# A decoder layer's expert retrieval: a shorter routing spread over the first expert half, and the first four queries computed with tokens on partitions

## Chip, cores and metric

One core of a Trainium2 chip runs the whole layer. The metric is the device time of one execution in microseconds (us); the median of three runs is given, and one more execution was profiled. The core's engines run side by side, each through its own queue in order: PE (matrix products and transposes), DVE (VectorE), ACT (ScalarE), POOL (GpSimd) and SP, which issues the transfers. PE's clock has two levels, 1.2 and 2.4 GHz; the profile gives the granted clock of a stretch as a share of the upper one.

## The reference

256 tokens of 1024 numbers go through a mixer (a state-space part and attention, one output projection), a layer norm, and a PEER sublayer, then a second norm. The change lies in the first norm and in PEER:

```python
h = _layernorm(DN_ALPHA * h + mix, ln1_g, ln1_b)
# PEER, per chunk of 128 tokens (8 heads, two key halves of 128 keys, top 16)
q = (xc @ w_q).reshape(TOKEN_CHUNK, 8, 2, 128)
s = jnp.einsum('thcd,hcnd->thcn', q, sub_keys)
s1, i1 = lax.top_k(s[:, :, 0], 16)
s2, i2 = lax.top_k(s[:, :, 1], 16)
cand = (s1[..., :, None] + s2[..., None, :]).reshape(TOKEN_CHUNK, 8, 256)
cidx = (i1[..., :, None] * 128 + i2[..., None, :]).reshape(TOKEN_CHUNK, 8, 256)
top, pos = lax.top_k(cand, 16)
eidx = jnp.take_along_axis(cidx, pos, axis=-1)
g = jax.nn.softmax(top, axis=-1)
act = jax.nn.gelu(jnp.einsum('td,thkd->thk', xc, expert_u[eidx]))
out = jnp.einsum('thk,thkd->td', g * act, expert_v[eidx])
```

There are 16384 experts, 16 heads-times-halves (called `hc`), all in float32.

## The kernel before

PEER is computed densely: all 16384 experts' products with all 256 tokens are formed, 128 experts at a time (128 `u` tiles, later 128 `v` tiles), and weighted by gates that are zero for experts not chosen. A float32 product is made of three float32r products. Each weight tile of 128 x 1024 is loaded by SP into one of four `raw` buffers; ScalarE rounds it to `hi` (L71, three buffers), and DVE or GpSimd forms the rest, `lo = raw - hi` (L72, three buffers). The normed tokens `xh`, `xl` are split in the same way, with features on partitions. `dense` (L995) then does 24 matmuls of 256 columns: 8 of (hi, xh), 8 of (hi, xl), 8 of (lo, xh).

The stages, in order:
- The norm runs over two blocks of 128 tokens. Block 0: ScalarE centres (L680), GpSimd scales (L681), DVE finishes `h1b` (L684), PE transposes it (L689), ScalarE writes `xh` (L690) and DVE `xl` (L698). Block 1 is the same, with DVE at L677 in place of ScalarE and GpSimd.
- The w_q loop over 16 `hc`: load, split (`lo` on GpSimd for every fourth, on DVE otherwise), `dense`, a copy `qT` by ScalarE (L756), two score matmuls against `keys` (L744), their copies `sco` (L745), and two `top16` on DVE. A `top16` is five operations on 128 values: MAX8, FIND_INDEX8, MATCH_REPLACE8, MAX8, FIND_INDEX8.
- The first half of `u`: 32 calls of `u_pair`, each two tiles and one Gelu of 128 x 512 by ScalarE (L769). The second tile's `lo` is GpSimd's. Between them `route(b)` forms, for each block, the 16 x 16 sums `cand` (L784), eight `top16` on 256 values, and turns the positions into the two key indices by comparisons with a ramp (`eq`, L799 to L804), then the softmax (L808 to L814). It is written one step after each pair, but a scheduler orders each engine's queue by when inputs are ready, and put nearly all of it ahead.
- The second half of `u` with the gates beside it, then the `v` tiles (L925), then the last norm.

Of the kernel before, what the change touches and what calls it, by code (L numbers as in the profile page):

```python
# [20 lines left out]
T = 256  # L21
# [32 lines left out]
def layer(ctx, tc, I, out, tap=None, upto=None):  # L54
# [19 lines left out]

    ident = const.tile([128, 128], F32, name="ident")
# [26 lines left out]

    with ExitStack() as px:
# [6 lines left out]
        with ExitStack() as mx:  # L110
            sb = mx.enter_context(tc.tile_pool(name="sb", bufs=1))
            def eng(g, i):
                return P if CFG[g][i] == "P" else V

            prm = sb.tile([128, 1088], F32, name="prm")
# [25 lines left out]
            U = sb.tile([128, NPAIR, 2, 32], F32, name="U")  # L141
# [142 lines left out]
            big = [sb.tile([128, 1024], F32, name=f"big{n}") for n in range(4)]  # L284
# [60 lines left out]
            def s5_c():  # L345
                tmp = [sb.tile([128, 1024], F32, tag=t, name="cp") for t in ("yT", "dU")]
                powers(Lam, 4, cre, cim, Cbd, 1, -1.0, (eng("cp", 0), eng("cp", 1)), tmp)
# [99 lines left out]
            def glu(yT):  # L447
                yv = yT.rearrange("p k b j c -> p k (b j c)")
                yh = sb.tile([128, 4, T], F32R, tag="big2", name="yh")
                yl = sb.tile([128, 4, T], F32R, tag="big3", name="yl")  # L450
# [97 lines left out]
            def do(w):  # L548
# [63 lines left out]
            if tap:  # L612
# [5 lines left out]
                   allow_small_or_imprecise_dtypes=True)  # L618

# [51 lines left out]
            def ln_apply(b):  # L671
                mean, nstd = st[b]
                z, h1 = gz[:, 2 + b], h1b[:, b]
                for c in range(2):
# [5 lines left out]
                    S.activation(h1[:, cs], z[:, cs], AF.Identity, bias=mean, scale=-1.0)  # L680
                    P.tensor_tensor(h1[:, cs], h1[:, cs], g1[:, 0, cs], op=OP.mult)  # L681
                for c in range(2):
                    cs = slice(512 * c, 512 * c + 512)
                    V.scalar_tensor_tensor(h1[:, cs], h1[:, cs], nstd, g1[:, 1, cs], op0=OP.mult,  # L684
                                           op1=OP.add)
# [4 lines left out]
                    S.copy(xh[:, 4 * c:4 * c + 4, 128 * b:128 * b + 128], pt)  # L690
# [15 lines left out]
            ln_apply(0)  # L706
            ln_stats(1)
# [3 lines left out]
            normed = st["low"]  # L711

# [9 lines left out]
    with ExitStack() as rx:  # L722
# [14 lines left out]
        PACE = lambda i: 1  # L737
        keys = sb.tile([128, 16, NK], F32, name="keys")
        nc.sync.dma_start(keys, I["keys"])
# [9 lines left out]
        late = None  # L749
        for hc in range(16):  # L750
            with tc.issue_after(normed.ins) if hc == 2 else ExitStack():
                hi, lo = split(load(I["w_q"][hc]), P if hc % 4 == 3 else V)
            pt = abank([128, 2, T])[:, 0]
            dense(PE, pt, hi, lo, xh, xl, xl if hc == 0 else lo)
            qT = sb.tile([128, T], F32, tag="qT", bufs=2, name="qT")
            S.copy(qT, pt)  # L756
            if late:
                scores(*late)
            late = hc, qT
        scores(*late)  # L760
# [3 lines left out]
        def u_pair(i):  # L764
            pt = sbank([128, 2, T])
            for r in range(2):
                hi, lo = split(load(I["u"][i + r]), P if r else V)
                dense(PE, pt[:, r], hi, lo, xh, xl)
            S.activation(act[0][:, i:i + 2], pt, AF.Gelu_apprx_tanh)  # L769
# [3 lines left out]
        i2n = sb.tile([128, 2, 128], F32, name="i2n")  # L773

        def route(b):
            for hc in range(EARLY, 16):
                yield top16(tops[b][:, hc], topi[b][:, hc], sco[:, b, hc], NK, "t1")
            topf = sb.tile([128, 16, TOPK], BF, tag="topf", bufs=1, name="topf")
            V.tensor_copy(topf, topi[b])
            cand = sb.tile([128, 8, 16, 16], F32, tag="c0", bufs=1, name="cand")  # L780
            tv = tops[b].rearrange("p (h c) k -> p h c k", c=2)
            fv = topf.rearrange("p (h c) k -> p h c k", c=2)
            sh = [128, 8, 16, 16]
            yield V.tensor_tensor(cand, tv[:, :, 0, :, None].to_broadcast(sh),  # L784
                                  tv[:, :, 1, None, :].to_broadcast(sh), op=OP.add)
            best = sb.tile([128, 8, 16], F32, tag="best", bufs=1, name="best")
# [7 lines left out]
            V.tensor_scalar(ab[:, 0], pos, 4, None, op0=OP.logical_shift_right)  # L794
            V.tensor_scalar(ab[:, 1], pos, 15, None, op0=OP.bitwise_and)
            yield V.tensor_copy(abf, ab)
# [10 lines left out]
            df = sb.tile([128, 8, 16], F32, tag="df", bufs=1, name="df")  # L807
            V.tensor_tensor(df, best, best[:, :, 0:1].to_broadcast([128, 8, 16]), op=OP.subtract)  # L808
            S.activation(df, df, AF.Exp)
            yield  # L810
            sm = sb.tile([128, 8], F32, tag="sm", bufs=1, name="sm")
            V.tensor_reduce(sm, df, axis=AX.X, op=OP.add)
            V.reciprocal(sm, sm)
            yield V.tensor_tensor(gn[:, b].rearrange("p (h k) -> p h k", k=16), df,  # L814
                                  sm[:, :, None].to_broadcast([128, 8, 16]), op=OP.mult)
            pt = sbank([128, 3, 128])
            for i, s in enumerate((i1n, i2n, gn)):
                PE.transpose(pt[:, i], s[:, b], ident)
            sl = slice(128 * b, 128 * b + 128)
            V.tensor_copy(i1T[:, sl], pt[:, 0])  # L820
            V.tensor_copy(i2T[:, sl], pt[:, 1])

            gr = sb.tile([128, 128], F32, tag="gr", bufs=1, name="gr")
            V.tensor_scalar(gr, pt[:, 2], GSC, None, op0=OP.mult)
            V.tensor_copy(gT[:, 0, sl], gr)
            yield V.tensor_sub(gT[:, 1, sl], gr, gT[:, 0, sl])
            if tap:
                tap(f"i1n{b}", i1n[:, b]); tap(f"gn{b}", gn[:, b])
# [6 lines left out]
        for _ in routing:  # L835
# [239 lines left out]
```

## Time and profile before

| what | us |
|---|---|
| runs: median (lowest to highest of 3) | 1005.85 (1005.19 to 1007.71) |
| profiled execution, its own time | 1009.14 |
| its span in the trace | 1007.4 |
| busy: PE, DVE, ACT, POOL | 965.5, 708.8, 453.4, 246.9 |

The span runs from the first to the last instruction that the profiler saw; the execution's own time has about 2 us around it. Busy times of engines overlap, and PE's is not time at its peak.

### The profile page before, as it was taken

Reading aid. Unit: us, or ns where it says so; the run is one execution under the profiler, and the core shown is the slowest. Engines: PE = TensorE matmul, PEld = TensorE weight load, DVE = VectorE, ACT = ScalarE, POOL = GpSimd, SP = SyncE. Lnnn points to the kernel's source line nnn. Section 1 sums busy time; section 2 is a strip of 40 time slices with the busy share of each in tenths; the row PEclk is TensorE's granted clock in tenths of the full one; section 3 lists DMA queues with packets and bytes.
Section 4 is the critical chain, followed back from the end, with each engine's and each line's share of the span. In section 5 each row is a group of like instructions: output and inputs, shape, how many; then the busy total and the mean of one; then the engine's idle time right before and its main releaser. Section 6 shows DMA issues by size and latency. Waiting matters only on the chain.

```text
span 1007.4 us, 16390 instructions
## 1 busy us (share of the span) xinstructions
PE 965.5 (96%) x6326; PEld 857.0 (85%) x6326; DVE 708.8 (70%) x1348; ACT 453.4 (45%) x736; POOL 246.9 (25%) x123
## 2 busy tenths in 40 slices
PE   7899997999889999999999999999999999999996
PEld 3776887999889999999999998978888888888884
DVE  8965577999993612597879999755555555555556
ACT  3214543545344444454444343554554455544552
POOL 2000010144543444345464564600000000000002
PEclk9999998999999999999999999999999999999998
DMA  8312354544446565544444443656666676666661
GB/s 334 105 43 63 95 178 168 162 151 149 149 145 198 167 199 173 165 147 147 147 147 122 133 145 126 209 176 199 190 190 196 196 262 202 190 199 193 191 194 55
DMA packets 46142, 166.24 MB, mean 165 GB/s; under 512 B 5232, under 2 KB 5232, under 8 KB 45936
## 3 DMA queue, kind: packets, MB, share of 16 engines
q1 hardware_dynamic: 46064, 165.20, 51.7%
q8 instruction: 49, 0.80, 0.3%
q14 instruction: 29, 0.24, 0.1%
HBM read 163.09 MB, written 2.10 MB: 164 GB/s over the span
## 4 chain that ended last, share of the span: by engine, by line
PE 71%; DVE 23%; DMA 2%; issue 1%; ACT 1%; SPq 0%; POOL 0%; DVEq 0%; ACTq 0%; POOLq 0%
PE pw L925 34%; PE psb L995 25%; DVE lo L72 5%; PE pw L162 2%; PE pw L873 2%; DVE o L868 2%; DVE act L880 2%; PE psb L151 2%; DVE tmp L732 1%; PE pw L630 1%; DVE o L865 1%; DVE topi L734 1%; DVE eq L801 1%; DMA w<-in_w_in 1%; DVE topi L731 1%
## 5 line engine op out<-in xcount | busy, mean ns | idle before, releaser
L71 ACT CAST hi<-raw 128x1024 fp32r<-128x1024 f32 x275 | 289.6, 1054 | 320.7 <-PE pw L925 164.5
L72 DVE TENSOR_TENSOR lo<-raw,hi 128x1024 fp32r<-128x1024 f32 x207 | 269.2, 1300 | 230.3 <-ACT hi L71 226.8
L72 POOL TENSOR_TENSOR lo<-raw,hi 128x1024 fp32r<-128x1024 f32 x68 | 179.6, 2643 | 184.1 <-ACT hi L71 119.0
L995 PE MATMUL psb<-xh,lo 128*128 128x256 f32 x1024 | 153.0, 289 | 9.9 <-DVE lo L72 9.5
L995 PE MATMUL psb<-xh,hi 128*128 128x256 f32 x1024 | 157.8, 290 | 2.5 <-ACT act L769 2.4
L995 PE MATMUL psb<-xl,hi 128*128 128x256 f32 x1024 | 154.3, 290 | 0.0
L925 PE MATMUL pw<-hi,wh 128*128 128x512 f32 x492 | 151.8, 389 | 1.0 <-ACT wh L845 1.0
L925 PE MATMUL pw<-hi,wl 128*128 128x512 f32 x492 | 152.1, 390 | 0.2
L925 PE MATMUL pw<-lo,wh 128*128 128x512 f32 x492 | 151.7, 389 | 0.0
L995 PEld LDWEIGHTS psb<-xh,lo 128*128 128x128 f32 x1024 | 133.5, 192 | 12.3 <-DVE lo L72 11.9
L995 PEld LDWEIGHTS psb<-xh,hi 128*128 128x128 f32 x1024 | 135.0, 191 | 4.0 <-ACT act L769 3.1
L995 PEld LDWEIGHTS psb<-xl,hi 128*128 128x128 f32 x1024 | 133.5, 192 | 0.0
L925 PEld LDWEIGHTS pw<-hi,wh 128*128 128x128 f32 x492 | 92.3, 188 | 20.5 <-ACT wh L845 1.4
L925 PEld LDWEIGHTS pw<-hi,wl 128*128 128x128 f32 x492 | 92.2, 188 | 20.3 <-DVE wl L846 1.1
L925 PEld LDWEIGHTS pw<-lo,wh 128*128 128x128 f32 x492 | 92.4, 188 | 19.1
L968 POOL TENSOR_TENSOR tail<-tail 128x512 f32<-128x512 f32 x2 | 2.5, 1294 | 345.7 <-ACT tail L967 345.7
L880 DVE SCALAR_TENSOR_TENSOR act<-pw,act 128x256 f32<-128x256 f32 x124 | 65.9, 588 | 20.3 <-PE pw L873 20.3
L883 ACT ACTIVATE act<-pw 128x256 f32<-128x256 f32 (+29 forms) x64 | 27.8, 434 | 102.3 <-DVE act L880 84.5
L873 PE MATMUL pw<-o,o 128*128 128x128 f16 x512 | 72.8, 225 | 0.7 <-DVE o L868 0.7
L909 POOL TENSOR_TENSOR act<-act,ga 128x512 f32<-128x512 f32 (+29 forms) x32 | 51.2, 1600 | 85.5 <-ACT ga L908 64.2
L868 DVE TENSOR_TENSOR o<-eq,gT 128x1024 f16<-128x1024 f16 x64 | 52.4, 855 | 0.1
L846 DVE TENSOR_TENSOR wl<-act,wh 128x256 fp32r<-128x256 f32 x123 | 51.3, 417 | 0.0
(274 smaller groups left out, 992.7 us busy)
## 6 DMA issues: line engine op xcount, KB each, us to landing
raw<-in_u SPq DMA_DIRECT2D x128, 512.0 KB, 3.6
raw<-in_v SPq DMA_DIRECT2D x128, 512.0 KB, 4.1
raw<-in_w_q SPq DMA_DIRECT2D x16, 512.0 KB, 4.1
w<-in_w_in SPq DMA_DIRECT2D x15, 512.0 KB, 8.6
raw<-in_w_out SPq DMA_DIRECT2D x8, 512.0 KB, 4.0
xT<-in_xT SPq DMA_DIRECT2D x4, 256.0 KB, 5.2
raw<-in_w_glu SPq DMA_DIRECT2D x2, 512.0 KB, 3.7
xn<-in_xn SPq DMA_DIRECT2D x2, 512.0 KB, 3.6
```

The source lines that it names most:

```text
L71: S.copy(hi, raw)
L72: eng.tensor_tensor(lo, raw, f32(hi), op=OP.subtract)
L151: PE.matmul(pt[b], xT[:, d, 128 * b:128 * b + 128], w[:, 512 * k:512 * k + 512], start=d == 0, stop=d == 7)
L162: PE.matmul(pt[m], w[:, c], xT[:, d], start=d == 0, stop=d == 7)
L846: V.tensor_sub(wl, act[half][:, i], f32(wh))
L868: V.tensor_tensor(o2[:, k], eq, over(gT[:, k, t]), op=OP.mult)
L873: PE.matmul(pt[:, i], o1[:, (q + i) // 2, :, i % 2], o2[:, k, (q + i) // 2, :, i % 2], start=k == 0, stop=k == 1)
L880: V.scalar_tensor_tensor(a, pt[:, :, HALF * h:HALF * h + n], 1.0 / GSC, a, op0=OP.mult, op1=OP.mult)
L883: S.activation(act[1][:, done:, tq].rearrange("p i t -> p t i"), pt[:, :, HALF + done:], AF.Copy, scale=1.0 / GSC)
L909: P.tensor_tensor(a[:, :, :m1], a[:, :, :m1], raw[:, :, :m1], op=OP.mult)
L925: PE.matmul(acc[b][c], x[:, tk], w[:, 512 * c:512 * c + 512], start=first and j == 0, stop=last and j == 2)
L995: PE.matmul(pt, w[:, 128 * d:128 * d + 128], x[:, d], start=n == 0 and d == 0, stop=n == 2 and d == ND - 1)
```

## The change

It does four things. The weights of the first four queries are loaded as W4 (four pieces of two input slices each, rows of 512 bytes), and `query4(b)` computes these queries for one block with tokens on partitions and the weights moving: 24 matmuls of 512 columns, a copy, four transposes back, a copy. The split of W4's last two pieces is put inside the norm: `hi` on ScalarE behind the centring, `lo` on GpSimd behind block 0's `h1b`. The routing works on 64 candidate pairs in place of 256, finds row and column by short operations, has ScalarE copy the indices out to full size (`fv`), and does one softmax for both blocks. Its 36 steps are tied to the first 26 pairs, each behind the pair's second `lo`; and all `lo` of the first `u` half are DVE's. `keys` is loaded earlier, and some buffers change places.

```diff
+    def split3(raw):
+        hi, lo = (stream.tile([128, 1024], F32R, tag=t, bufs=n, name=t)
+                  for t, n in (("hi", HIB), ("lo", LOB)))
+        S.copy(hi, raw)
+        return hi, lo, V.tensor_tensor(lo, raw, f32(hi), op=OP.subtract)
...
+            W4 = []
+            for q in range(4):
+                raw = stream.tile([128, 1024], F32, tag="raw", bufs=RAWB, name="raw")
+                for k in range(2):
+                    c = 256 * q + 128 * k
+                    st["dma"] = nc.sync.dma_start(
+                        raw[:, 512 * k:512 * k + 512].rearrange("p (h c) -> p h c", h=4),
+                        I["w_q"][0:4, :, c:c + 128].rearrange("h p c -> p h c"))
...
+            def query4(b):
+                tk = slice(128 * b, 128 * b + 128)
+                pt = abank([128, 512])
+                for j, (x, y) in enumerate(((xh, 0), (xh, 1), (xl, 0))):
+                    for d in range(8):
+                        PE.matmul(pt, x[:, d, tk], W4[d // 2][y][:, 512 * (d % 2):512 * (d % 2) + 512],
+                                  start=j == 0 and d == 0, stop=j == 2 and d == 7)
+                qe = late.tile([128, 512], F32, tag="qe", bufs=2, name="qe")
+                S.copy(qe, pt)
+                pt = pbank([128, 4, 128])
+                for i in range(4):
+                    PE.transpose(pt[:, i], qe[:, 128 * i:128 * i + 128], ident)
+                S.copy(qf[:, :, tk], pt)
+
+            for q in range(2):
+                high4(q)
+                low4(q, V)
...
             ln_apply(0)
+
+
+            for q in range(2, 4):
+                with tc.issue_after(st["cen"].ins):
+                    high4(q)
+                tc.add_manual_dep(low4(q, P).ins, st["h1"].ins.name,
...
+            query4(0)
+            query4(1)
...
-        for hc in range(16):
-            with tc.issue_after(normed.ins) if hc == 2 else ExitStack():
-                hi, lo = split(load(I["w_q"][hc]), P if hc % 4 == 3 else V)
+        todo = [(hc, qf[:, hc]) for hc in range(4)]
+        for hc in range(4, 16):
+            raw = load(I["w_q"][hc])
...
         def u_pair(i):
             pt = sbank([128, 2, T])
             for r in range(2):
-                hi, lo = split(load(I["u"][i + r]), P if r else V)
+                hi, lo, low = split3(load(I["u"][i + r]))
                 dense(PE, pt[:, r], hi, lo, xh, xl)
...
-            cand = sb.tile([128, 8, 16, 16], F32, tag="c0", bufs=1, name="cand")
+            cand = sb.tile([128, 8, 64], F32, tag="c0", bufs=1, name="cand")
...
+            for n, (i0, i1, w, o) in enumerate(((0, 1, 16, 0), (1, 4, 8, 16), (4, 8, 4, 40), (8, 16, 1, 56))):
...
-                yield top16(best[:, h], pos[:, h], cand[:, h].rearrange("p a b -> p (a b)"), 256, "t2")
+                yield top16(best[:, b, h], pos[:, h], cand[:, h], 64, "t2")
...
+                fv = sb.tile(sh, BF, tag="fv", bufs=2, name="fv")
+                S.copy(fv, iv[:, :, c, :, None].to_broadcast(sh))
...
-                yield V.tensor_tensor(eq, eq, fv[:, :, c, :, None].to_broadcast(sh), op=OP.mult)
+                yield V.tensor_tensor(eq, eq, fv, op=OP.mult)
...
-        routing = chain(route(0), route(1))
-        for i in range(0, HALF, 2):
-            u_pair(i)
-            for _ in range(PACE(i)):
-                next(routing, None)
+        steps, last = chain(route(0), route(1)), weigh()
+        STEPS, PAIRS, GAP = 36, 26, 2
+        done = 0
+        for n in range(HALF // 2):
+            low, ac = u_pair(2 * n)
+            with tc.issue_after(low.ins), tc.issue_after(ac.ins) if n >= PAIRS else ExitStack():
+                while done < min(STEPS, -(-STEPS * (n + 1) // PAIRS)):
```

How it moves instructions is seen at three places. (Names carry buffer numbers; the numbers are those of the build.) PE's queue of before, from the last matmuls of the output projection (`W`, `mixh`) through the norm's transposes (`ident`, `h1b`) to the third query:

```order
L630 MATMUL pw<-W_1063,mixh 128x512
L689 MATMUL psb<-ident,h1b 128x128 x16
L995 MATMUL pa<-xh,hi 128x256 x8
L995 MATMUL pa<-xh,lo 128x256 x8
L995 MATMUL pa<-xl,hi 128x256 x8
L995 MATMUL pa<-xh,hi 128x256 x8
```

The same place after the change (`W_1092` and `W_1096` are W4's first two pieces, `hi` and `lo` its last two; L747 is `query4`):

```order
L705 MATMUL psb<-ident,h1b 128x128 x8
L747 MATMUL pa<-W_1092,xh 128x512 x2
L747 MATMUL pa<-W_1096,xh 128x512 x2
L747 MATMUL pa<-hi,xh 128x512 x4
L747 MATMUL pa<-W_1092,xh 128x512 x2
L747 MATMUL pa<-W_1096,xh 128x512 x2
L747 MATMUL pa<-lo,xh 128x512 x4
L747 MATMUL pa<-W_1092,xl 128x512 x2
L747 MATMUL pa<-W_1096,xl 128x512 x2
L747 MATMUL pa<-hi,xl 128x512 x3
L705 MATMUL psb<-ident,h1b 128x128 x4
```

Block 0's `query4` now stands between the transposes of the two blocks, where nothing stood. ScalarE's queue at the same time after the change, from the centring on; before, `xh` followed the centring directly:

```order
L696 ACTIVATE h1b_1086<-gz_1081,mv_1142 128x512 x2
L736 CAST hi_1100<-raw_1097 128x1024
L736 CAST hi_1105<-raw_1102 128x1024
L706 CAST xh_1087<-psb_1188 128x4x128
L706 CAST xh_1087<-psb_1195 128x4x128
L826 CAST hi_1328<-raw_1325 128x1024
```

The two `hi` of W4 stand ahead of block 0's `xh`. DVE's queue after the change, at the end of block 0's and block 1's last `top16` of queries (`tops_1321` and `tops_1322`), the four parts of `cand`, and `lo` of the fourth `u` tile (L79, `lo_2124`):

```order
L805 MAX_INDEX topi_1323<-tops_1321,tmp_1995 128x8
L803 MATCH_REPLACE tmp_2004<-tops_1322,sco_1320 128x128
L867 TENSOR_TENSOR cand_2078<-tops_1321 128x8x16
L804 MAX tops_1322<-tmp_2004 128x8
L867 TENSOR_TENSOR cand_2078<-tops_1321 128x8x24
L805 MAX_INDEX topi_1324<-tops_1322,tmp_2004 128x8
L867 TENSOR_TENSOR cand_2078<-tops_1321 128x8x16
L867 TENSOR_TENSOR cand_2078<-tops_1321 128x8x8
L79 TENSOR_TENSOR lo_2124<-raw_2121,hi_2123 128x1024
L801 MAX best_2014<-cand_2078 128x8 x2
```

And there before, where `lo_2185` is that of the fifth tile, the fourth being GpSimd's:

```order
L779 CAST topf_2107<-topi_1222 128x256
L733 MAX tops_1221<-tmp_2036 128x8
L784 TENSOR_TENSOR cand_2109<-tops_1220 128x2048
L734 MAX_INDEX topi_1223<-tops_1221,tmp_2036 128x8
L730 MAX best_2173<-cand_2109 128x8
L72 TENSOR_TENSOR lo_2185<-raw_2182,hi_2184 128x1024
```

All 32 `top16` of the queries stand ahead of the fourth tile's `lo` after the change; 9 other `lo` stand between the first of them and it (six of w_q, three of `u`). Before, 10 of DVE's stood between the first `top16` and the fifth tile's.

## Rows read from the trace of the kernel before

**Rows 1.** The page: the chain that ended last, by line.
```profile
PE pw L925 34%; PE psb L995 25%; DVE lo L72 5%; PE pw L162 2%; PE pw L873 2%; DVE o L868 2%; DVE act L880 2%; PE psb L151 2%; DVE tmp L732 1%; PE pw L630 1%; DVE o L865 1%; DVE topi L734 1%; DVE eq L801 1%; DMA w<-in_w_in 1%; DVE topi L731 1%
```

**Rows 2.** Windows: length; busy PE, PEld, DVE, ACT, POOL (x instructions); clock, DMA share, GB/s.
```profile
165.60:218.80 53.20, 53.20 (x449) 53.05 (x449) 51.62 (x265) 27.36 (x63) 13.15 (x6) 1.00 0.50 162
218.80:304.30 85.50, 75.89 (x601) 73.85 (x600) 85.19 (x185) 38.08 (x44) 39.99 (x13) 0.98 0.43 142
...
413.50:530.00 116.50, 116.39 (x1047) 110.20 (x1045) 96.11 (x152) 57.34 (x97) 58.85 (x31) 1.00 0.48 146
```

**Rows 3.** Timeline of line 769: count, least/median/most ns, first and last start.
```profile
L769 ACT ACTIVATE act<-psb x32: 586/591/601, 220.0 to 413.2; 128x512 f32<-128x512 f32 x32
```

**Rows 4.** Timeline, ScalarE, 392 to 414: start, us, engine, line, operation.
```profile
407.43 0.59 ACT L769 ACTIVATE act<-psb 128x512 f32<-128x512 f32 x1
```

**Rows 5.** Timeline of the norm, 146 to 167; in brackets idle before, releaser.
```profile
146.31 1.34 ACT L680 ACTIVATE h1b<-gz,mv 128x512 f32<-128x512 f32 x2 [6.02 <-DVE mv L1007]
...
149.22 1.70 DVE L684 SCALAR_TENSOR_TENSOR h1b<-h1b,w,gz 128x512 f32<-128x512 f32 x2
...
151.21 1.07 ACT L690 CAST xh<-psb 128x512 fp32r<-128x512 f32 x2 [3.56 <-PE psb L689]
...
153.49 0.74 DVE L677 SCALAR_TENSOR_TENSOR h1b<-gz,mv,ng 128x512 f32<-128x512 f32 x1
...
156.23 1.42 DVE L684 SCALAR_TENSOR_TENSOR h1b<-h1b,w,gz 128x512 f32<-128x512 f32 x2
...
157.13 1.94 PE L689 MATMUL psb<-ident,h1b 128*128 128x128 f32 x8 [5.49 <-DVE h1b L684]
...
165.14 2.39 POOL L72 TENSOR_TENSOR lo<-raw,hi 128x1024 fp32r<-128x1024 f32 x1 [15.43 <-DMA keys<-in_keys]
```

**Rows 6.** A window at the first query, columns as in rows 2.
```profile
159.00:163.40 4.40, 4.40 (x25) 4.40 (x25) 2.38 (x3) 0.59 (x1) 0.00 (x0) 0.59 0.61 195
```

**Rows 7.** The chain that ended last, a piece of the v phase.
```profile
828.88 168.49 PE pw L925 x742
```

**Rows 8.** Timeline, 240 to 249.5.
```profile
240.24 4.44 POOL L72 TENSOR_TENSOR lo<-raw,hi 128x1024 fp32r<-128x1024 f32 x1 [2.66 <-ACT hi L71]
242.34 3.42 DVE L72 TENSOR_TENSOR lo<-raw,hi 128x1024 fp32r<-128x1024 f32 x1
...
246.40 0.31 ACT L809 ACTIVATE df<-df 128x128 f32<-128x128 f32 x1 [4.94 <-DVE df L808]
```

**Rows 9.** Groups by shape, 165 to 305: busy us, mean ns, idle before.
```profile
L71 ACT CAST hi<-raw 128x1024 fp32r<-128x1024 f32 x43 | 44.8, 1048 | 63.7 <-PE psb L995 17.5 <-PE pa L995 15.8 <-DMA raw<-in_u 11.5
...
L744 PE MATMUL pw<-keys,qT 128*128 128x128 f32 x64 | 9.8, 276 | 0.0
...
L730 DVE MAX8 tops<-sco 128x8 f32<-128x128 f32 x32 | 7.7, 279 | 0.0
...
L730 DVE MAX8 best<-cand 128x8 f32<-128x256 f32 x16 | 6.6, 413 | 0.0
```

**Rows 10.** Timeline, DVE, 165 to 182.
```profile
171.02 1.21 DVE L72 TENSOR_TENSOR lo<-raw,hi 128x1024 fp32r<-128x1024 f32 x1
172.14 0.48 DVE L730 MAX8 tops<-sco 128x8 f32<-128x128 f32 x2
...
174.63 1.21 DVE L72 TENSOR_TENSOR lo<-raw,hi 128x1024 fp32r<-128x1024 f32 x1
```

**Rows 11.** Timeline, DVE, 213 to 258.
```profile
219.88 2.27 DVE L784 TENSOR_TENSOR cand<-tops 128x2048 f32<-128x2048 f32 x1
...
222.67 1.20 DVE L72 TENSOR_TENSOR lo<-raw,hi 128x1024 fp32r<-128x1024 f32 x1
```

**Rows 12.** Timeline, SyncE, 125 to 165: first issue, us to the last.
```profile
129.88 9.56 SPq L64 DMA_DIRECT2D raw<-in_w_q  x6
```

**Rows 13.** The page: a queue (packets, MB, share of 16 engines), issues (KB, us to landing).
```profile
q1 hardware_dynamic: 46064, 165.20, 51.7%
...
raw<-in_w_q SPq DMA_DIRECT2D x16, 512.0 KB, 4.1
```

More of the change, by code (lines that the diff above doesn't have):

```diff
@@ L283, in layer @@
             Kin = sb.tile([128, NPAIR, 128], F32, name="Kin")
-            big = [sb.tile([128, 1024], F32, name=f"big{n}") for n in range(4)]
+            big = [se.tile([128, 1024], F32, name=f"big{n}") for n in range(4)]
             rot = sb.tile([128, 2, NPAIR, NCH], F32, name="rot")
@@ L618, in layer @@
                    allow_small_or_imprecise_dtypes=True)
+            early.close()
+            late = px2.enter_context(tc.tile_pool(name="late", bufs=1, side="right"))
+            keys = late.tile([128, 16, NK], F32, name="keys")
+            qf = late.tile([128, 4, T], F32, name="qf")
             po = [[pbank([128, 512]) for _ in range(2)] for _ in range(2)]
@@ L706, in layer @@
             ln_apply(0)
+            for q in range(2, 4):
+                with tc.issue_after(st["cen"].ins):
+                    high4(q)
+                tc.add_manual_dep(low4(q, P).ins, st["h1"].ins.name,
+                                  mybir.DependencyInfo(mybir.DependencyClass.Sync,
+                                                       mybir.DependencyReason.DATA),
+                                  reason="GpSimd after the first norm")
             ln_stats(1)
@@ L747, in scores @@
                     top16(tops[b][:, hc], topi[b][:, hc], sco[:, b, hc], NK, "t1")
[L749 to L752 removed]
+        todo = [(hc, qf[:, hc]) for hc in range(4)]
+        for hc in range(4, 16):
+            raw = load(I["w_q"][hc])
+            if hc == 4:
+                with tc.issue_after(w4dma.ins):
+                    nc.sync.dma_start(keys, I["keys"])
+            hi, lo = (stream.tile([128, 1024], F32R, tag=t, bufs=n, name=t)
+                      for t, n in (("hi", HIB), ("lo", LOB)))
+            with tc.issue_after(cast.ins) if hc == 4 else ExitStack():
+                S.copy(hi, raw)
+            with tc.issue_after(normed.ins) if hc == 4 else ExitStack():
+                (P if hc % 4 == 3 else V).tensor_tensor(lo, raw, f32(hi), op=OP.subtract)
             pt = abank([128, 2, T])[:, 0]
[L754 removed]
+            dense(PE, pt, hi, lo, xh, xl)
             qT = sb.tile([128, T], F32, tag="qT", bufs=2, name="qT")
             S.copy(qT, pt)
[L757 to L760, printed above, removed]
+            scores(*todo.pop(0))
+            if len(todo) > 1:
+                scores(*todo.pop(0))
+            todo.append((hc, qT))
+        for t in todo:
+            scores(*t)
+        px2.close()
         if tap:
@@ L835, in layer @@
-        for _ in routing:
+            V.tensor_tensor(gn.rearrange("p b (h k) -> p b h k", k=16), df,
+                            sm[:, :, :, None].to_broadcast([128, 2, 8, 16]), op=OP.mult)
+            yield
+            for b in range(2):
+                pt = sbank([128, 3, 128])
+                for i, s in enumerate((i1n, i2n, gn)):
+                    PE.transpose(pt[:, i], s[:, b], ident)
+                sl = slice(128 * b, 128 * b + 128)
+                V.tensor_copy(i1T[:, sl], pt[:, 0])
+                V.tensor_copy(i2T[:, sl], pt[:, 1])
+                gr = sb.tile([128, 128], F32, tag="gr", bufs=1, name="gr")
+                V.tensor_scalar(gr, pt[:, 2], GSC, None, op0=OP.mult)
+                V.tensor_copy(gT[:, 0, sl], gr)
+                V.tensor_sub(gT[:, 1, sl], gr, gT[:, 0, sl])
+                if tap:
+                    tap(f"i1n{b}", i1n[:, b]); tap(f"gn{b}", gn[:, b])
+                yield
@@ new lines, in layer @@
+        steps, last = chain(route(0), route(1)), weigh()
[5 more added lines that the diff above has]
+                while done < min(STEPS, -(-STEPS * (n + 1) // PAIRS)):
+                    done += 1
+                    next(steps, None)
+                if n == PAIRS - 1:
+                    assert next(steps, 0) == 0
+                if n >= PAIRS + GAP - 1:
+                    next(last, None)
@@ L836, in layer @@
+        for _ in last:
             pass
```

99 lines of the change are left out of this document (57 added, 42 removed).

## The prediction

> **What bounds the kernel now.** The page's busy times come first: PE is at work nearly the whole span, so a gain must come from work taken from PE or from a place where PE stands still, and a total does not say where. The chain that ended last does: it is PE's two big loops and, as the largest piece off PE, DVE's `lo` subtraction of L72 [rows 1]. The windows by stage give the places [rows 2]. From 165.60 to 218.80 PE is busy for all 53.20 us while DVE is at 51.62: both full. From 218.80 to 304.30 the roles turn: DVE is busy 85.19 of 85.50, PE only 75.89. So the routing, all at the front of the first u half, starves PE there.
>
> The Gelu of each pair of tiles is a clock for that half. There are 32, from 220.0 to 413.2 [rows 3]. The last two, undisturbed, lie 5.76 apart (407.43 [rows 4] to 413.19): 2.88 per tile, 0.12 per 256-column matmul (24 per tile). 31 such pairs would take 178.6 and took 193.2: **14.6 us are stalls.**
>
> The second hole is the norm. Behind block 0's transposes PE has nothing until `h1b` of block 1 comes, 5.5 us [rows 5], and then the granted clock is 0.59 until 163.4 [rows 6]: the first dense matmuls run near the lower of the two levels (1.2 and 2.4 GHz). The second query, 2.88 more, is done at about 166.3.
>
> **The change part by part.**
>
> *Queries on token partitions.* 24 matmuls of 512 columns per block, at the pitch of the v phase (168.49/742 = 0.227 [rows 7]), are 5.45 a block and 10.9 for both, against 4 x 2.88 = 11.5 for four dense blocks: little saved in work, the place changes. Block 0's group can start when the first half of its `xh` is written, about 151.85 [rows 5]. Its first 8 need only `hi`: to 153.7. The next 8 need `lo` of weights 2 and 3 from GpSimd, which may begin when block 0's last `h1b` ends (149.22 + 1.70 = 150.92) and take 2.4 each: to 153.35 and 155.8 [rows 5]. So this group ends near 156.3 and the third near 158.1: PE is fed through the hole, with a gap of 2 us inside.
>
> *GpSimd's two subtractions inside the norm.* DVE's first block-1 operation with two SBUF inputs (L677) starts at 153.49 [rows 5], just behind the start of the second GpSimd subtraction. What that costs is seen at 242.34: a DVE `lo` took 3.42 instead of 1.2 while GpSimd's ran from 240.24 for 4.44 [rows 8]; each waited the other out. By that row L677 waits until 155.8, 2.3 late. Bounds: 0 if the two miss each other, 4.7 if DVE waits for both. I take 2.3, since the start times leave one collision. A rule speaks against this edit: the Trainium skill, "SBUF — State Buffer", section "Who interferes with whom", has a DVE instruction with two SBUF inputs and a GpSimd instruction that reads SBUF shut each other out for a whole instruction. The trace agrees (3.42 beside 1.2 [rows 8]); by the rule a collision costs up to one subtraction, 2.4, by the row 2.2, and the sum is the same by either.
>
> So the second `h1b` of block 1 ends at 157.65 + 2.3 = 159.9, and block 1's group starts at about 160.4 at the full clock, ending at 160.4 + 5.45 + 0.5 (four transposes of `qe`) = 166.35. **Four queries are done where before two were.**
>
> *The w_q loop.* Dense block 4 with the other `qe` transposes ends at 166.35 + 2.88 + 0.5 = 169.7; four score matmuls (0.276 [rows 9], some 0.24 where they overlap) end at 170.7, and DVE's first `top16` starts at 171.0. PE alone would do 11 more dense blocks (31.7) and 28 scores (6.7): first u tile at 209.1.
>
> *DVE until the fourth u tile.* This decides the forecast. Between 171.02 and 174.63 lie one `lo` of 1.12 and two `top16` [rows 10]: (3.61 - 1.12)/2 = 1.245 a `top16`. The order has 32 `top16`, 9 `lo` and 4 small `cand` additions (0.28, as other operations on 128 values [rows 9]) ahead of the `lo` of u tile 3: 171.0 + 39.8 + 10.1 + 1.1 = 222.0, its end 223.1. The same count on the kernel before, from 171.02 on (30 `top16` 37.4, ten `lo` 11.2, `cand` 2.2), gives 221.8 for a `lo` that the trace has at 222.67, the `topf` cast between [rows 11]. PE wants this `lo` at 209.1 + 3 x 2.88 + 16 x 0.12 = 219.7, so **one stall of 3.4 us remains**, and tile 3 ends at 223.1 + 0.96 = 224.1.
>
> *The rest of the half.* A pair gives DVE two `lo` (2.24) and 1.4 steps. The `top16` on 64 wide is not in the trace: 0.41 an operation for 256 and 0.28 for 128 [rows 9] make about 0.21, and 0.9 to 1.0 a step; bounds 0.6 (a quarter of the 256-wide) and 1.25 (no better than 128-wide). The heaviest steps are the 2048-element `eq` operations, at most 2.27, as the addition of that size [rows 11]. So a pair needs 3.6 to 5.5 of its 5.76, with nothing on GpSimd to collide with: PE sets the pace, and the 31 `lo` that GpSimd loses (34.7 on DVE) are paid from idle time. 60 tiles x 2.88 = 172.8 follow: last Gelu at 224.1 + 172.8 + 0.1 = **397.0 against 413.2, 16.2 us earlier**.
>
> *The `fv` casts on ScalarE* (128 x 2048) are not in the trace; two 128 x 1024 casts of 1.05 [rows 9] say 2.1, and twice that if the broadcast read is slow. The first waits for the last `topi` of block 0 (220.2), with `hi` of tile 4, the first Gelu, the second `fv` and `hi` of tile 5 queued behind it. At 2.1 these `hi` come at 223.35 and 227.1, and PE wants them at 224.1 and 227.0: free. At 4.2 the last comes at 231.3, 4.3 late. I take free; the row is the same engine and operation. One softmax for both blocks saves two of four table loads, for which no tile waits later in the half: nothing.
>
> *W4 in 512-byte runs.* ScalarE comes to `hi` of weights 2 and 3 at 147.65 (146.31 + 1.34) and has two casts (2.1) to do ahead of the `xh` at 151.21 [rows 5], so the fourth piece may land until 149.1. Issues begin where w_q's did, 129.88 [rows 12]: 2 MB in 19.2 us asks 109 GB/s; one w_q load moved 512 KB in 4.1 us, 128 GB/s, beside others [rows 13]. No row has such packets. Lower bound: by bytes, free. Upper bound: each costs what a packet costs now, 0.517 x 16 x 1007.4 / 46064 = 0.18 us [rows 13]; 4096 packets on 16 engines then take 46 us. I take free, since that average is of packets seven times as long. The Trainium skill, "DMA: Bandwidth & Descriptors", section "Why small descriptors are slow (HBM only)", has a fixed overhead of 3 cycles per packet, beside 16 for 512 bytes of data; no run here shows it, and by it the sum stays.
>
> *After the half.* Gate work that ran early now lies at its end; from 413.50 to 530.00 DVE is at 96.11 of 116.50 [rows 2], 20 us free to take it. Nothing.
>
> **Sum.** 16.2 off: span 1007.4 to 991.2, execution 1009.14 to 992.9. The profiled execution lies 3.3 above the median of the runs, so the forecast in runs is 1005.85 - 16.2 = **989.7**. Of the 16.2, 11.2 (14.6 - 3.4) is the half's stall, the rest the norm and queries.
>
> **The rivals.**
> - *Neither stall nor collision.* If GpSimd and L677 miss each other, 2.3 more; if the DVE count is 7% high, the 3.4 goes too: 984.0.
> - *The lock takes both.* Block 1's norm waits for both subtractions, another 2.4: 992.1. For it, the wait of 242.34 [rows 8]; against it, DVE may enter between the two.
> - *ScalarE behind `topi`.* The casts are slow or later than counted: 4 to 7 lost, 993.7 to 996.7. For it: ScalarE sat 4.94 for DVE's `df` at 246.40 [rows 8].
> - *The stall moves.* DVE carries all `lo`, steps bunch at a pair, and 8 to 14 us return: 998 to 1004. For it: DVE was at 85.19 of 85.50. Against it: spread out, the half's DVE work is 64 x 1.12, 15 for `top16` and some 35 for the index steps (estimated from [rows 9, 11]), 122 us of 176.
> - *W4 late (slower).* Every us behind 149.1 shifts all that follows, for `xh` stands behind the casts in ScalarE's queue. At 165.3 (59 GB/s) the gain is gone; at the upper price the piece lands at 129.9 + 46 = 176, 27 late: 1016.5.
> - *It does nothing:* PE is bound throughout and the stalls only show elsewhere; 2 in 100, since PE's missing 9.6 us in 218.80 to 304.30 are real [rows 2].
>
> **How the numbers follow.** Chances: forecast 0.54 (988 to 991.5), neither 0.09, lock 0.12, ScalarE 0.10, moved stall 0.07, W4 late 0.06, nothing 0.02. The range reaches from the first rival to the lower edge of the moved stall: 984 to 998. Within 0.3% (3 us) no measurement here tells a change from none. The first four cases are faster, and 0.03 of the moved stall; 0.05 (the rest of it, and nothing) ends within 3 us; late W4 and a worst moved stall, 0.07, end slower.
>
> **What would show it.** Gelus 5.76 apart from the second pair on, the last near 397; one PE wait of about 3 us for DVE's `lo` near 220; matmuls of `query4` from 151.9 with a gap near 154 to 156, and a granted clock of 1.00 at 160; a lengthened DVE operation beside GpSimd's second `lo`; no GpSimd work from 210 to the second half. The forecast is wrong if W4's casts wait for a DMA after 149, if DVE is full past 230, or if PE waits for `hi` near 224.

## The result and the profile after

The changed kernel took 997.52 us (median of 4 runs, 997.19 to 999.71) against 1006.78 (1005.19 to 1008.49): ratio 0.9912, interval 0.9889 to 0.9936. Measured again beside the last experiments (run e12), it was 0.9878 (0.9858 to 0.9898). So it is faster, by 9 to 12 us where 16 were forecast, and inside the range, 0.5 us below its upper edge. The profiled execution's span is 997.9.

The page of the changed kernel, busy time by engine and the chain by engine and line:

```profile
PE 965.8 (97%) x6286; PEld 855.0 (86%) x6286; DVE 714.9 (72%) x1396; ACT 459.0 (46%) x737; POOL 161.5 (16%) x92
...
PE 81%; DVE 17%; issue 1%; ACT 0%; DVEq 0%
```

Work moved from GpSimd (246.9 before) to DVE. The Gelu line, now 848, as [rows 3]; then PE's waits over the first u half, in total, times and longest, in the kernel before (205 to 420) and in the changed one (205 to 400):

```profile
L848 ACT ACTIVATE act<-psb x32: 587/597/600, 224.1 to 402.8; 128x512 f32<-128x512 f32 x32
```

```profile
PE psb L995 <- DVE lo L72: 7.3, 6, 2.3
PE psb L995 <- ACT act L769: 2.4, 2, 2.0
PE psb L995 <- POOL lo L72: 0.2, 1, 0.2
```

```profile
PE psb L1111 <- DVE lo L79: 4.3, 1, 4.3
PE psb L1111 <- ACT act L848: 0.4, 1, 0.4
```

One long wait is left where there were several, and it is the one that was named: tile 3's `lo`. The windows on it and behind it, columns as in [rows 2]:

```profile
222.00:226.40 4.40, 0.11 (x2) 0.05 (x1) 4.40 (x23) 4.40 (x5) 0.00 (x0) 1.00 0.00 0
226.40:229.80 3.40, 3.40 (x17) 3.40 (x18) 3.40 (x18) 2.52 (x4) 0.00 (x0) 0.52 0.50 154
```

PE stands 4.3 us, and then works 3.4 us at a granted clock of 0.52, the lower of the two levels: half of that, 1.6 us, is lost again. The last Gelu came 10.4 earlier than before, not 16.2.

Part of the rest lies where the change is not. The granted clock in the mixer, in two windows where nothing of the code was changed, first of the kernel before, then of the profiled changed one, then of the second profile of the same changed kernel (run e12):

```profile
30.00:40.00 10.00, 10.00 (x56) 8.87 (x55) 9.89 (x25) 4.40 (x8) 0.00 (x0) 0.85 0.06 11
70.00:80.00 10.00, 10.00 (x36) 5.47 (x36) 8.75 (x14) 0.68 (x4) 0.00 (x0) 0.83 0.00 0
```

```profile
30.00:40.00 10.00, 10.00 (x50) 8.77 (x49) 9.88 (x25) 4.49 (x8) 0.00 (x0) 0.73 0.01 2
70.00:80.00 10.00, 10.00 (x34) 5.63 (x33) 9.53 (x17) 1.61 (x8) 0.00 (x0) 0.68 0.00 0
```

```profile
30.00:40.00 10.00, 10.00 (x56) 8.87 (x55) 9.88 (x25) 4.39 (x8) 0.00 (x0) 0.86 0.07 12
70.00:80.00 10.00, 10.00 (x35) 5.51 (x36) 8.68 (x14) 0.61 (x4) 0.00 (x0) 0.83 0.00 0
```

0.12 and 0.15 of 10 us each are 2.7 us of full-clock work, and in the first profile the norm and the first u half indeed lie 2.7 later than in e12 (the last Gelu 402.8 against 400.1). Steps are therefore compared with e12, whose mixer ran like that of the kernel before: its span is 995.0, 12.4 under 1007.4, and its last Gelu is at 400.1.

### The profile page after: what moved, and what is told of

Read it like the earlier page. It is cut to its first block, busy times and chain, and to the rows that moved or that the text cites. A ratio compares the mean times of both kernels' runs of the same rounds, so it can differ in the third digit from the quotient of the medians.

```text
span 997.9 us, 16315 instructions
## 1 busy us (share of the span) xinstructions
PE 965.8 (97%) x6286; PEld 855.0 (86%) x6286; DVE 714.9 (72%) x1396; ACT 459.0 (46%) x737; POOL 161.5 (16%) x92
## 4 chain that ended last, share of the span: by engine, by line
PE 81%; DVE 17%; issue 1%; ACT 0%; DVEq 0%
PE pw L1041 35%; PE psb L1111 29%; PE pa L1111 3%; PE pw L173 3%; DVE lo L72 2%; DVE o L984 2%; DVE act L996 2%; PE pw L989 2%; PE pw L646 2%; PE psb L162 2%; DVE o L981 1%; PE pw L517 1%; DVE eq L982 1%; PE pw L392 1%; PE psb L446 1%
## 5 line engine op out<-in xcount | busy, mean ns | idle before, releaser
L72 DVE TENSOR_TENSOR lo<-raw,hi 128x1024 fp32r<-128x1024 f32 x163 | 211.3, 1296 | 152.8 <-ACT hi L71 148.3
L71 ACT CAST hi<-raw 128x1024 fp32r<-128x1024 f32 x195 | 206.1, 1057 | 200.1 <-PE pw L1041 166.4
L1041 PE MATMUL pw<-hi,wh 128*128 128x512 f32 x492 | 151.9, 389 | 1.0 <-ACT wh L961 1.0
L79 DVE TENSOR_TENSOR lo<-raw,hi 128x1024 fp32r<-128x1024 f32 x64 | 78.1, 1221 | 57.1 <-ACT hi L78 57.1
L72 POOL TENSOR_TENSOR lo<-raw,hi 128x1024 fp32r<-128x1024 f32 x32 | 83.0, 2592 | 218.0 <-ACT hi L71 202.5
L78 ACT CAST hi<-raw 128x1024 fp32r<-128x1024 f32 x64 | 66.9, 1047 | 89.5 <-PE psb L1111 81.3
```

The source lines that it names most:

```text
L71: S.copy(hi, raw)
L72: eng.tensor_tensor(lo, raw, f32(hi), op=OP.subtract)
L78: S.copy(hi, raw)
L79: return hi, lo, V.tensor_tensor(lo, raw, f32(hi), op=OP.subtract)
L1041: PE.matmul(acc[b][c], x[:, tk], w[:, 512 * c:512 * c + 512], start=first and j == 0, stop=last and j == 2)
```

## The experiments

The ratios are to the kernel before, on the same chip and in the same rounds. The changed kernel's own, 0.9878, is from e12, which ran on the chip of e9 to e11; e1 to e8 ran on two others, so small differences between the groups are left to the traces. Expected times in us are on the scale of the changed kernel's 997.5. "Gelu" is always the last one of the first u half. Where times of events are compared, the mixer's clock was alike unless said otherwise. The second u half, whose own code no experiment changes, took about 3 us less in the profiles of e1, e7 and e9 than in most others (last section); so the traces are compared up to the last Gelu.

**e1: the two late `lo` on GpSimd.**
```diff
-    def split3(raw):
+    def split3(raw, eng=V):
...
-        return hi, lo, V.tensor_tensor(lo, raw, f32(hi), op=OP.subtract)
+        return hi, lo, eng.tensor_tensor(lo, raw, f32(hi), op=OP.subtract)
...
-                hi, lo, low = split3(load(I["u"][i + r]))
+                hi, lo, low = split3(load(I["u"][i + r]), P if r and i < 4 else V)
```


> The changed kernel with the lo of u tiles 1 and 3 (the second tiles of the first two pairs) on GpSimd again, all else as changed. Theory (DVE's queue is what tile 3 waits for, and the low clock behind that one wait is part of its price): GpSimd has tile 3's lo by 217, the 4.3 us wait and about 1.8 us of half-clock matmuls behind it go, a wait under 0.5 us for tile 4's lo remains; about 991.6 against 997.5. Rival (the stall only moves to the next lo on DVE): DVE's queue is shorter by one lo only, 1.1 us, and the wait reappears at tile 4: 995.5 to 996.5.

0.9862 (0.9838 to 0.9886), mixer as before, Gelu 399.0. The wait for `lo` is gone, and another stands there. PE's waits from 205 on, and ScalarE's timeline:

```profile
PE psb L1111 <- ACT act L848: 2.8, 2, 2.5
```

```profile
211.48 1.05 ACT L78 CAST hi<-raw 128x1024 fp32r<-128x1024 f32 x1 [1.53 <-PE psb L1111]
220.10 1.90 ACT L896 CAST fv<-topi 128x2048 bf16<-128x2048 uint32 x1 [7.57 <-DVE topi L805]
221.91 1.04 ACT L78 CAST hi<-raw 128x1024 fp32r<-128x1024 f32 x1
222.85 0.59 ACT L848 ACTIVATE act<-psb 128x512 f32<-128x512 f32 x1
```

ScalarE stood 7.57 us for DVE's last `topi`, with the first Gelu behind `fv`. That is the rival "ScalarE behind `topi`", hidden in the changed kernel under DVE's longer wait. The ratio alone, 992.9 on the scale of the expectation, would speak for the theory. The trace speaks for the rival: the stall moved, to the first Gelu and not to tile 4's `lo`, and the last Gelu is only 1.1 before e12's. The other 3.3 of the 4.4 by which the span is shorter (990.6 against 995.0) lie in the second u half.

**e2: W4's last two `lo` on DVE, ahead of the norm** (`for q in range(4)` in place of `range(2)`, and the part with `range(2, 4)` left out).

> The changed kernel with all four W4 pieces split ahead of the norm, the last two lo on DVE in its idle time before block 0's statistics, none on GpSimd. Theory (the shared access of GpSimd and DVE holds block 1's first operation 2.2 us, and all that follows shifts by that): that operation takes 0.74 again, everything behind is about 2.2 us earlier, 995.3 against 997.5. Rival (DVE is late for other reasons, or two more lo ahead of the norm delay it): within 0.7 us of 997.5, or slower.

0.9877 (0.9851 to 0.9902), no better than the changed kernel. The theory's first half held: in e12 block 1's first operation is held, the timelines of GpSimd and DVE; in e2 it is not:

```profile
150.54 4.74 POOL L740 TENSOR_TENSOR lo<-raw,hi 128x1024 fp32r<-128x1024 f32 x2 [1.43 <-PE pw L646]
```

```profile
152.88 2.95 DVE L693 SCALAR_TENSOR_TENSOR h1b<-gz,mv,ng 128x512 f32<-128x512 f32 x1
155.81 0.73 DVE L693 SCALAR_TENSOR_TENSOR h1b<-gz,mv,ng 128x512 f32<-128x512 f32 x1
```

```profile
152.88 0.74 DVE L693 SCALAR_TENSOR_TENSOR h1b<-gz,mv,ng 128x512 f32<-128x512 f32 x1
153.61 0.75 DVE L693 SCALAR_TENSOR_TENSOR h1b<-gz,mv,ng 128x512 f32<-128x512 f32 x1
```

The first `top16` came at 168.55 instead of 170.49, tile 3's `lo` at 220.31 instead of 222.33, and PE went on 2.0 earlier (221.59 against 223.60). But a wait of 4.2 us for tile 3 stayed, and the lower clock behind it lasted longer; the windows in e12 and in e2:

```profile
223.60:227.00 3.40, 3.40 (x17) 3.40 (x18) 3.40 (x18) 2.52 (x4) 0.00 (x0) 0.54 0.53 154
```

```profile
221.60:227.00 5.40, 5.40 (x25) 5.40 (x26) 5.40 (x33) 2.60 (x4) 0.00 (x0) 0.50 0.62 187
```

The 32 matmuls behind the wait, 3.84 at 0.12 each, took 5.43 in e12 and 6.45 in e2. That took back half of the 2.0, and the Gelu gained 1.0.

**e3 and e4: each half of the change alone.** e3 keeps W4, `query4` and the 12-query loop, with all of `u_pair` and `route` as before; e4 keeps the routing, `split3` and `weigh`, on the 16-query loop.

> Only the first part of the change: W4, query4 and the 12-query loop, with the routing, u_pair and softmax of the kernel before. Theory (from the first top16 on DVE sets the time, and it starts 2.5 us later than before because its work of four queries arrives late): PE's 5 us lead is not used; 1006 to 1010, no gain against 1006.8. Rival (the queries' lead on PE is a gain of its own, as the forecast's split of 11.2 and 5 has it): about 1001.5 to 1002.

> Only the other part: the shorter, spread routing, all lo of the first u half on DVE and one softmax, on the 16-query loop of the kernel before. Theory (DVE's queue reaches tile 3's lo at 222 as in the changed kernel, but PE wants it only at 224.7, so no wait is left): all 14.6 us of stall go, less some 2 us for gate work moved behind the half: 993 to 994.5, faster than the whole change. Rival (the parts add up as forecast, 11 of 16): slower than the whole change by 3 to 5 us, 1000.5 to 1002.5.

e3: 1.0021 (1.0003 to 1.004), no gain and rather a loss. e4: 0.9875 (0.9852 to 0.9899), all of the whole change's gain. PE's waits from 205 to 420, in e3:

```profile
PE psb L1074 <- DVE lo L72: 14.8, 7, 4.6
PE psb L1074 <- ACT act L848: 2.3, 2, 1.9
```

In e4, from 166 to 420, no `lo` is waited for:

```profile
PE pw L916 <- DVE o L911: 0.4, 1, 0.4
PE psb L1038 <- ACT act L775: 0.4, 1, 0.4
```

In e3, whose mixer ran as before, PE starts the u half earlier (first Gelu 214.3 against 220.0), but DVE's first `top16` starts later, 170.21 against 168.54 before, and DVE sets the pace from there: the last Gelu is 2.4 later, at 415.55. In e4, whose mixer was clocked as in the first profile, tile 3's `lo` starts at 223.05, 2 us earlier than there (225.07), and PE, later with its queries, comes for it at 226.4: no wait, and no low clock behind one. Its last Gelu, 401.3, is 1.5 before the first profile's.

**e5 and e6: `fv` behind its pair's Gelu.** e5 is e1 with the edit below, e6 adds e2.
```diff
-            with tc.issue_after(low.ins), tc.issue_after(ac.ins) if n >= PAIRS else ExitStack():
+            with tc.issue_after(low.ins), tc.issue_after(ac.ins):
```


> As e1 (lo of u tiles 1 and 3 on GpSimd), and each step's ScalarE work, the fv casts, queued behind the Gelu of its own pair for all pairs, not for the last ones alone. Theory (in e1 the wait only changed its place: PE stood 2.5 us for the first Gelu, which sat behind fv and its wait for DVE's last topi; with fv gone from there nothing stops PE): Gelus 5.76 apart from the first one near 215, the last near 394.5 where e1 had 399.0; ratio to the kernel before about 0.982. Rival (the wait moves on to tile 4's or 5's lo, since DVE's queue is as long as it was): a DVE wait of 2 us or more near 222 and no better than e1's 0.986.

> e5 and e2 together: W4 split ahead of the norm, the lo of tiles 1 and 3 on GpSimd, fv behind the Gelus. Theory: the first top16 on DVE at 168.5 as in e2, no wait of over 1 us in the first u half, the last Gelu near 392.4 (20.8 before that of the kernel before), ratio about 0.980. Rival (the shared access was not on the path once the DVE wait is gone): the same as e5.

e5: 0.9849 (0.9832 to 0.9865); e6: 0.9836 (0.9818 to 0.9855), both with the mixer clocked as in the first profile. The rival of e5 holds: ScalarE's wait is gone, and in both PE waits 2.1 us for tile 4's `lo`. DVE in e6:

```profile
213.75 2.57 DVE L79 TENSOR_TENSOR lo<-raw,hi 128x1024 fp32r<-128x1024 f32 x1
...
224.05 1.22 DVE L79 TENSOR_TENSOR lo<-raw,hi 128x1024 fp32r<-128x1024 f32 x1
```

Behind tile 2's `lo` (held by GpSimd's beside it, 2.57 for 1.2) stand the last `top16` and `cand`, and tile 4's only then. DVE's queue itself is too long, whichever `lo` is taken off it.

e6's theory failed too (Gelu 398.9 where 392.4 was expected; some 2.7 of that is the mixer's, as between the two profiles of the changed kernel), and its rival, "the same as e5", has the number but not the reason. The first `top16` came 1.7 earlier than in e5 (171.49, 173.15) and PE went on 1.7 earlier behind its wait (225.32, 227.00). Then the matmuls ran at the lower clock in e6 and not in e5, behind waits of the same 2.1 us, and 0.2 was left at the last Gelu. The windows in e5 and in e6:

```profile
227.00:230.40 3.40, 3.40 (x28) 3.40 (x29) 3.40 (x25) 1.05 (x1) 0.00 (x0) 1.00 0.46 154
```

```profile
226.30:229.70 3.40, 3.40 (x19) 3.40 (x19) 3.37 (x23) 0.10 (x1) 0.00 (x0) 0.53 0.67 186
```

**e7 and e8: what the rest of the routing's edits do.** e7 gives every second `lo` of the half to GpSimd (`i < 64` in e1's edit). e8 drops the ties of the steps to the pairs.
```diff
-            with tc.issue_after(low.ins), tc.issue_after(ac.ins) if n >= PAIRS else ExitStack():
+            with ExitStack():
```


> The changed kernel with the lo of every second u tile on GpSimd throughout the first half, as the kernel before had it. Theory (32 more lo on DVE were paid from its idle time, and shared with GpSimd its idle time also takes the collisions): the same as e1 within 1.5 us, whose first two it contains; single DVE operations with two SBUF inputs take 2 to 3.4 us. Rival (collisions are what the changed kernel avoided by taking all lo on DVE): Gelus further apart than 5.76 among the routing steps, 4 to 8 us behind e1.

> The changed kernel without the ties that spread the routing steps over the pairs; the scheduler places them by when their inputs are ready. Theory (shorter routing alone is not enough, the spreading is a good part of the gain): the steps run ahead of the lo of the first ten pairs, and PE loses 6 to 12 us there; 1003 to 1009. Rival (the routing is now so short that its place does not matter): within 2 us of the changed kernel's 997.5.

e7: 0.9967 (0.9945 to 0.9989), three quarters of the gain gone, 1% behind e1; the rival is right, with some 10 us where it said 4 to 8. Single operations show why, as GpSimd's and DVE's lie over each other:

```profile
242.98 2.44 POOL L79 TENSOR_TENSOR lo<-raw,hi 128x1024 fp32r<-128x1024 f32 x1 [10.22 <-DVE best L801]
243.30 3.21 DVE L898 TENSOR_TENSOR eq<-abf,iotal 128x2048 bf16<-128x2048 bf16 x1
```

A 1.21 us compare took 3.21. Between 232.78 and 288.44 eight pairs took 55.7 us where 46.1 would do, 9.6 more; the stretched DVE operations there (that compare, two `lo`, a 0.28 us step that took 2.50, three additions that took 3.57 where e12 has 1.47) add up to about 9. The routing steps also ran earlier (140 DVE instructions in that stretch for 70 in e12), and ScalarE's `fv` waited 6.7 and 3.5 us for DVE; in e8, with such waits of 3.3 and 2.5 but all `lo` on DVE, that cost PE nothing. So that DVE has all `lo` is one part of the change that its gain hangs on. What it would give with the old, longer routing, no run here shows.

e8: 0.9892 (0.9873 to 0.9911), the same as the changed kernel, and my theory is wrong. Behind the 4.3 us wait for tile 3, PE has no wait from 228 to 300 although the steps run early, window 231 to 275:

```profile
231.00:275.00 44.00, 44.00 (x369) 44.00 (x368) 43.86 (x163) 25.78 (x28) 0.00 (x0) 1.00 0.58 177
```

DVE is full (43.86 of 44.00) and PE too. The routing is short enough that its place costs nothing.

**e9 to e12: the backlog itself.** e9 moves the `top16` of the last four queries (8 of 32) behind the first tiles, with e5's `fv` edit:
```diff
-        EARLY = 16
+        EARLY = 12
...
-        STEPS, PAIRS, GAP = 36, 26, 2
+        STEPS, PAIRS, GAP = 44, 26, 2
```
e10 adds e2; e11 is e10 with PAIRS = 22; e12 is the changed kernel once more.

> The changed kernel with the top16 of the last four queries (8 of the 32) turned into routing steps, 44 steps over the same 26 pairs, and the fv casts behind the Gelu of their own pair; GpSimd's two lo inside the norm stay, none in the u half. Theory (what is late for tile 3 is DVE's backlog of the first four queries' top16, about 10 us, which the early queries hand over at once while DVE takes 3.61 per query against PE's 3.36): without these 8 ahead of it tile 3's lo comes by 212 and PE never waits in the half; Gelus 5.76 apart from the first near 215, last near 394.5, ratio to the kernel before about 0.982. Rival (some other wait, the scheduler's order or ScalarE, takes its place): no better than 0.985, with a wait of 2 us or more before 235.

> e9 with W4 split ahead of the norm as in e2. Theory: with PE as the only bound from the norm on, the 2.2 us of the held block-1 operation are 2.2 us of the whole: last Gelu near 392.3, ratio about 0.980. Rival (they were slack): the same as e9 within 0.5 us.

> e10 with the 44 steps over 22 pairs instead of 26, so that the softmax and the gates' transposes come four pairs earlier. Theory (the 0.9 us between the last two Gelus and the 0.9 behind them are the gate work that stands at the half's end): the last pair 5.76 behind the one before, about 1 us better than e10. Rival (two or three steps a pair are more than DVE can hide): stalls inside the half, 1 to 3 us worse than e10.

> The changed kernel itself once more, on the chip of e9 to e11 and in their rounds, so that the ratios compare. Theory: ratio 0.989 to 0.991; in its trace the 4.3 us wait for tile 3's lo and the half-clock matmuls behind it as before, and the first top16 at 171.1 or 173.2, with the two levels of the granted clock in the mixer deciding which. Rival (the first measurement was off): outside of that.

e9: 0.9828 (0.9805 to 0.9852), the theory, also in time: Gelu 394.0 where 394.5 was expected. Its Gelu line, and the window from the half's beginning:

```profile
L848 ACT ACTIVATE act<-psb x32: 597/597/600, 214.4 to 394.0; 128x512 f32<-128x512 f32 x32
```

```profile
213.00:304.00 91.00, 91.00 (x760) 91.00 (x760) 69.25 (x202) 45.06 (x50) 0.00 (x0) 1.00 0.62 190
```

PE is busy for all 91 us at the upper clock, with DVE at 69. e10: 0.9807 (0.9783 to 0.9831); the intervals overlap, but the traces, both with the mixer as before, agree with the theory up to the last Gelu: first `top16` 168.65 against 170.38, Gelu 392.2 against 394.0, all of the lead, where e2 kept half of it. (The profiled spans are the other way, 987.3 against 985.7, by the second u half.) e11: 0.9788 (0.9762 to 0.9814), not told apart from e10. Its last pair is 5.76 behind the one before, as expected:

```profile
362.47 0.60 ACT L841 ACTIVATE act<-psb 128x512 f32<-128x512 f32 x1
369.17 0.60 ACT L841 ACTIVATE act<-psb 128x512 f32<-128x512 f32 x1
375.87 0.60 ACT L841 ACTIVATE act<-psb 128x512 f32<-128x512 f32 x1
...
387.39 0.60 ACT L841 ACTIVATE act<-psb 128x512 f32<-128x512 f32 x1
393.15 0.60 ACT L841 ACTIVATE act<-psb 128x512 f32<-128x512 f32 x1
```

In e10 PE's transposes of the gates (three for each block) stand in the last pair for one block and right behind it for the other. In e11 both stand further ahead, and each adds 0.94 to its pair's 5.76: they cost it wherever they stand. So the last Gelu is 0.95 later than e10's; what follows it is 1.75 shorter, and the span 0.8, where about 1 was expected. e9, e10 and e11 beat both kernels.

## Why the prediction was right or wrong

- *The range: held by 0.5 us, and in part by luck.* None of the cases named ahead gives 997.5: ScalarE's ends at 996.7, the moved stall begins at 998. The forecast's own case reached to 991.5.
- *The place of the gain: right.* Gelus 5.76 apart on the mean from 232.12 to 393.39 (e12, 28 pairs), one wait for tile 3's `lo`, and no starving behind it.
- *The norm: right.* `query4` begins at 151.32 in e12 (forecast 151.9), and PE's gaps from there to block 1's transposes are 0.5 us (for GpSimd's second `lo`; a gap of 2 was forecast) and 1.0 (for block 1's `h1b`). The clock there, which was 0.59 before [rows 6]:

```profile
159.00:163.40 4.40, 4.40 (x26) 3.50 (x25) 2.76 (x4) 2.15 (x4) 0.00 (x0) 1.00 0.29 119
```

- *The count on DVE: right* in e12. First `top16` 170.49 (forecast 171.0), tile 3's `lo` at 222.33 (222.0), the wait 4.3 (3.4):

```profile
170.49 0.49 DVE L801 MAX8 tops<-sco 128x8 f32<-128x128 f32 x2 [0.82 <-ACT sco L813]
...
222.33 1.22 DVE L79 TENSOR_TENSOR lo<-raw,hi 128x1024 fp32r<-128x1024 f32 x1
```

- *The price of that wait: the step that failed*, "one stall of 3.4 us remains, and tile 3 ends at 223.1 + 0.96". I took the wait at its length and the matmuls behind it at 0.12. They ran at 0.52 to 0.54 of the clock for 3.4 us, 1.6 more. [Rows 6] had shown this behind the 5.5 us gap of the norm (0.59), and I used it there alone. It is not a fixed price: 0.1 to 2.6 us were lost in this way in the runs (last section).
- *Gate work behind the half, taken at nothing*: 0.95 at the last pair, which is one block's transposes, and 0.7 behind the last Gelu, where the other block's now stand; in e11 each costs 0.94 further ahead as well. The window read for "20 us free" ended at 530. Behind it DVE was full already before, and PE waited 2.2 us for its `lo`, before and after alike:

```profile
533.00:623.00 90.00, 87.39 (x772) 82.04 (x770) 89.93 (x105) 34.64 (x69) 52.28 (x24) 1.00 0.40 129
```

- In e12 the last Gelu came 3.1 later than forecast (400.1 for 397.0): 0.5 because PE got tile 3's `lo` at 223.6 and not at 223.1, 1.6 by the clock, 0.95 by the transposes. With the 0.7 behind it this is the 3.8 between 16.2 and 12.4. The first profile's other 2.9 is mainly the mixer's clock.
- *"Of the 16.2, 11.2 is the half's stall, the rest the norm and queries": wrong.* The queries alone lose 2 us (e3) and the routing alone has the whole gain (e4). PE's lead went into the wait at tile 3, because DVE, not PE, set the time from the first `top16` to there, and that began later: in e12 the way from the first `top16` to the last Gelu is 15.0 shorter than before (229.6 for 244.65), and it begins 1.95 later (170.49 for 168.54). My count contained this; the sentence did not draw it. e9 and e10 give the lead its worth: taking DVE's backlog away brought 0.9878 to 0.9828 and then 0.9807.
- *The lock: right in size* (2.2 for 2.3), and the rule of the Trainium skill, "SBUF — State Buffer", section "Who interferes with whom", agrees with it: 2.95 beside 0.73 for the same operation. It is on the path with a late DVE too: without it PE went on 2.0 earlier behind the wait in e2 and 1.7 in e6, but the clock behind the wait took back 1.0 and 1.5. In e10, with no wait, all of it reached the last Gelu.
- *`fv` on ScalarE: 1.90 for 2.1, right; "free" held by cover only.* e1 shows the wait under it.
- *W4: right.* In the first profile the casts of the last two pieces start at 149.67 with no wait for a DMA; the first two waited under 1 us (0.92 and 1.08 in e12):

```profile
137.49 1.05 ACT L736 CAST W<-raw 128x1024 fp32r<-128x1024 f32 x1 [0.93 <-DMA raw<-in_w_q]
139.20 1.05 ACT L736 CAST W<-raw 128x1024 fp32r<-128x1024 f32 x1 [0.66 <-DMA raw<-in_w_q]
...
149.67 1.99 ACT L736 CAST hi<-raw 128x1024 fp32r<-128x1024 f32 x2
```

- *The moved stall: not of the size named (8 to 14 us) in the changed kernel, but on a small scale in every attempt to remove the one wait* (e1, e5, e6), until the queue ahead of it was shortened (e9).

## What to carry to other kernels

A lead on the engine that seems to be the bound is worth nothing while the next engine's queue, counted from its own first operation, ends later: count that queue to the first result that is waited for, and shorten it there. A wait on TensorE can be dearer than its length: behind waits of 2.1 to 4.3 us here the lower clock cost 0.1 to 2.6 us more. So give it a term of its own with a range, and look at the granted clock behind the wait before a small gain or loss is put down to the edit. And when one wait is removed, look at what else stands in the queues at the same moment: the second and the third wait ended within 2 us of where the first had.

## What the runs showed of the hardware

- The mixer's granted clock fell into one of two patterns in executions whose operations there are the same: 0.83 to 0.89 and 0.83 to 0.84 in the two windows above (the kernel before, e1 to e3, e9 to e12) or 0.73 to 0.75 and 0.68 to 0.70 (the first profile, e4 to e7), with e8 between. Between the two profiles of the changed kernel that made 2.7 us. What set it is open: one execution's profile can't tell a smaller difference without these windows.
- The second u half, where the runs differ at most by the gate work at its beginning, also came in two forms. In 11 of the 14 profiles PE waits 2.2 us for DVE's `lo` there, with DVE full; in e1, e7 and e9 it does not, and from the last Gelu to the end these take 591.5 to 591.8 us where the others take 593.4 to 595.4. Whether that goes with the kernel or with the execution is open. PE's waits for DVE from 415 to 635 in e12, then in e9, and DVE's load in 100 us of it:

```profile
PE psb L1111 <- DVE lo L72: 2.2, 2, 1.1
PE pw L989 <- DVE o L984: 0.7, 2, 0.4
```

```profile
PE pw L989 <- DVE o L984: 0.7, 2, 0.4
```

```profile
520.00:620.00 100.00, 97.10 (x857) 91.02 (x856) 99.33 (x120) 38.53 (x78) 57.56 (x26) 1.00 0.40 132
```

```profile
514.00:614.00 100.00, 99.33 (x886) 94.16 (x886) 92.63 (x126) 43.49 (x86) 62.59 (x28) 1.00 0.47 144
```

- The price of a wait of PE in the clock behind it was not fixed: over the 24 or 32 matmuls behind it, 1.6 us more than at 0.12 each behind waits of 4.3 (both profiles of the changed kernel, and e8), 2.5 (e1) and 2.1 us (e6), 2.6 behind 4.2 (e2), 0.1 behind 2.1 (e5).
- A top-16 operation shrinks little with its width: 0.41 us at 256, 0.28 at 128, 0.22 at 64. The estimate of 0.21 held.
